# A gated linear attention layer with a convolutional FFN: the first unit ordered by need, row squares in place, and the up operands' splits later and behind loads

## The chip, the cores and the metric

The kernel runs on one core of one Trainium2 chip. The metric is the device time of one execution in microseconds; the time of a kernel is the median of its runs.

## The reference

With a depth of one, only the first mixer of the reference runs. The whole computation, in fp32, on a sequence of 2048 rows of 1024:

```
h = rmsnorm(x, mix_norm_w)
proj = h @ gla_w_in                       # 1024 -> q 512, k 512, v 1024, r 1024, gate rank 16
q, k, v, r, glr = split(proj)
log_a = log_sigmoid(glr @ w_gate2 + b_gate) / 16
g = cumsum(log_a) in chunks of 64 rows    # 4 heads, dk 128, dv 256
k_dec = k * exp(g_end - g)
for each chunk:  state = state * exp(g_end) + k_dec^T v ;  o = (q * 128**-0.5) @ state
o = rms_normalize(o) * gla_norm_w * silu(r)
x = x + o @ gla_w_out
h = rmsnorm(x, ffn_norm_w)
u = causal_dwconv(h @ w_up, conv_w, conv_b)      # 2 x 2816 columns, 3 taps
x = x + (silu(g) * val) @ w_down                 # g, val = halves of u
return rmsnorm(x, final_norm_w)
```

## The kernel before

**Arithmetic.** Every fp32 operand of a product is split into a high part (a copy to fp32r) and a low part (operand minus high part); a product is then three matmuls, high x low, low x high and high x high (`mm3p`, lines 179 to 189, matmuls at 184 to 186). `split` (191 to 194) makes the parts: the copy on ScalarE (line 193), the difference on VectorE (line 194). The large products are multiplied by blocks in seven products instead of eight, p1 to p7, which need sums and differences of blocks of both operands.

**Stages.** The rows are taken as pairs of 128-row tiles (e, d). Stage R projects r, A and B project k, q and v of two heads each and run the recurrence, Y is the output projection with the residual, U the up projection with convolution and gate, D the down projection and the last norm. One `unit(ps_, j)` is the seven products of stage `ps_` for row pair j, in the order p1, p5, p6, p2, p7, p3, p4. The host passes x a second time in transposed blocks (`xt`); each is multiplied by the norm weight on VectorE (`blocks_x`, line 461), while the factor of each row is applied after the product. That factor comes from `squares` (426): half a row tile is squared on ScalarE with its sum accumulated (line 434), and for the second half GpSimd adds the two sums (439), scales and adds epsilon (440) and takes the power -1/2 (441) into `rs`. The squares themselves go to a bf16 tile `junk` that nobody reads. Each call of `squares` issues the load of the half tile two further on (`load_rows`, 422) from ScalarE; the loads use two buffers.

**What sets the order.** The program is written down in one order; a scheduler then places each engine's instructions by that order and by when it takes operands to be ready, so an instruction written later can be issued earlier on its engine. Engines and queues run in the order placed. `tc.issue_after(ins)` places what is written in its block behind `ins` on the same engine, without waiting for it. Within the writing, a clock counts the products (`adv`, 0.227 us for a matmul of 512 columns, three to a step of `mm3p`), and `later_do(us, fn)` has `fn` written down once that clock has moved on by `us`; `need(...)` writes it down at once if it is wanted sooner.

**The first unit** (`first_pair`, 964 to 1124) does stage R for pair 0 with eight plain products, since the sums of blocks aren't there yet. SP's queue issues, in this order: the norm weight, the two transposed tiles (two halves each), the weight blocks, the 16 gate columns (`graw`, line 526, runs of 64 bytes), six copies of the second gate weight (`w2raw`, 546), its bias to all partitions (`bg`, 548), the third weight block, two further transposed tiles and two half rows. `blocks_x` for tiles 0 and 1, the masks of the recurrence (`masks`, 503) and the gate operands are written ahead of the first weight split. Then splits of weights (`weight`, 1009) and rows (`row`, 1001) alternate with products (`product`, 1060). The fourth weight block is loaded by ScalarE's queue into the buffers of the first two transposed tiles. Meanwhile `sum5`, `sum6` and `sum7` build the sums for p5, p6, p7 and p3, and `diffs` those of the rows.

**The up operands.** During the last unit of Y, after each product, `load_op(0, o)` (942) loads one operand of U for the first half of the rows, in SP's queue, in two transfers of 512 KB, and has its `halves` (950) written down `NLS` = 8.0 later by the clock: two splits of 128x1024. U itself (`phase_u`, 1254) begins when Y's last product has been written; it writes the splits of the first three up weights (`prep`, 1267; tile `uw`), then multiplies, operand by operand in the order p1, p5, p6, p7, p4, p2, p3, two column tiles each, and calls `need` for the operand before its first product.

Of the kernel before, what the change touches and what calls it, by code (L numbers as in the profile page):

```python
# [16 lines left out]
P = 128  # L17
# [8 lines left out]
def hybrid_kernel(  # L26
# [44 lines left out]
    NLY, NLE = 5.5, 9.0  # L71
    NLS = 8.0
    Y0, Y1, U0, U1 = 3.0, 2.8, 14.0, 11.0
# [117 lines left out]
    def split(hi, lo, src):  # L191

        order["act"] = nc.scalar.copy(hi, src)  # L193
        nc.vector.tensor_sub(lo, src, f32(hi))  # L194

# [228 lines left out]
    sq = {"n": 0}  # L424

    def squares():

        t, i = divmod(sq["n"], 2)
        r = xrow.pop(sq["n"])
        if i == 0:  # L430
            sq["ssq"] = small("ssq", f"ssq_a{t}", 2)
        ssq = sq["ssq"]
        junk = gp.tile([P, 1024], BF16, tag="cp", name=f"junk_{t}_{i}", bufs=4)
        nc.scalar.activation(junk[:, :512], r, AF.Square, accum_out=ssq[:, i:i + 1])
        load_rows(sq["n"] + 2, nc.scalar)
        sq["n"] += 1
        if i == 1:
            var = small("var", f"var_a{t}")
            nc.gpsimd.tensor_add(var, ssq[:, 0:1], ssq[:, 1:2])
            nc.gpsimd.tensor_scalar(var, var, 1.0 / D, EPS, op0=ALU.mult, op1=ALU.add)  # L440
            nc.gpsimd.tensor_tensor(rs[:, t:t + 1], var, neghalf, op=ALU.pow)
# [4 lines left out]
    def diff(j, o, a, c):  # L446
# [3 lines left out]
        return d  # L450

    def blocks_x(t):
        xb = xin.pop(t)
        bs = []
        for k in range(2):
            if t < 2:
                b = rp["p"].tile([P, 512], F32, tag="s2k", name=f"hb_{t}_{k}", bufs=SB)
            else:
                b = hb_tile(f"hb_{t}_{k}")
            w = nwt[:, HK * k:HK * (k + 1)].unsqueeze(2).to_broadcast([P, HK, P])  # L460
            nc.vector.tensor_tensor(b.rearrange("p (a c) -> p a c", c=P), xb[:, k, :].rearrange("p (a c) -> p a c", c=P), w, op=ALU.mult)
            bs.append(b)
        hsrc["t", t] = bs
        j = t // 2
        if t % 2 == 0:
            hsrc[j, "p1"], hsrc[j, "p2"] = bs
            return
        if j == 0:
# [32 lines left out]


    def masks():
        rp["later"] = rp["p"].tile([P, P], F32R, name="later")

        later_f = rp["p"].tile([P, 512], F32, tag="s2k", name="later_f", bufs=SB)
        nc.gpsimd.memset(later_f[:, :P], 1.0)
        nc.gpsimd.affine_select(
            out=later_f[:, :P], in_=later_f[:, :P], compare_op=ALU.is_gt, fill=0.0,
            base=0, pattern=[[-1, P]], channel_multiplier=1,  # L510
        )
        nc.gpsimd.memset(later_f[CH:P, 0:CH], 0.0)

        nc.gpsimd.memset(later_f[0:CH, CH - 1:CH], 1.0)
        nc.gpsimd.memset(later_f[CH:P, P - 1:P], 1.0)
        nc.vector.tensor_copy(rp["later"], later_f[:, :P])
        nc.vector.tensor_add(lastrow, ident[:, CH - 1:CH], ident[:, P - 1:P])

    def gate_weights():

        GR = 2 * RANK
        rp["wg"] = wg = rp["h"].tile([P, KT, GR], F32R, name="wg")
        rp["wgx"] = wgx = rp["h"].tile([P, KT, GR], F32R, name="wgx")
        graw = rp["p"].tile([P, 512], F32, tag="s2k", name="graw", bufs=SB)
        gv = graw[:, :KT * RANK].rearrange("p (a b) -> p a b", b=RANK)
        nc.sync.dma_start(gv, wv[:, :, OR + H * DV:OR + H * DV + RANK])
        nc.vector.tensor_copy(wg[:, :, :RANK], gv)
        nc.vector.tensor_sub(wg[:, :, RANK:GR], gv, f32(wg[:, :, :RANK]))

        def others():  # L530

            gx_ = graw[:, KT * RANK:2 * KT * RANK].rearrange("p (a b) -> p a b", b=RANK)
            nc.vector.tensor_add(gx_[:, :HK], gv[:, :HK], gv[:, HK:])
            nc.vector.tensor_scalar(gx_[:, HK:], gv[:, :HK], -1.0, 0.0, op0=ALU.mult, op1=ALU.add)
# [3 lines left out]
        later_do(24.0, others)  # L538

    def gate_weights2():  # L540


        rp["w2s"] = w2s = rp["p"].tile([P, 512], F32R, name="w2s")
        w2raw = rp["p"].tile([P, 512], F32, tag="s2k", name="w2raw", bufs=SB)
        for i in range(6):
            nc.sync.dma_start(w2raw[i * RANK:(i + 1) * RANK, :], w_gate2)
        rp["bg"] = rp["p"].tile([P, 512], F32, name="bg")
        nc.sync.dma_start(rp["bg"], b_gate.partition_broadcast(P))

        def parts():  # L550
            nc.vector.tensor_copy(w2s[0:96, :], w2raw[0:96, :])
# [412 lines left out]
    def first_pair():  # L964
# [17 lines left out]
        s_ = stage("p7", ((0, 0),))[:, HK:, :]  # L982
        stage("p6", ((1, 1), (1, 0)))
        fetch((0, 0))
        xin[1] = load_xt(1, 2)
        fetch((1, 0))
        gate_weights()
        gate_weights2()
        fetch((1, 1))
        xin[2], xin[3] = load_xt(2), load_xt(3)  # L990
        for m in range(2):
            load_rows(m, nc.sync)
        for t in range(2):
# [66 lines left out]
        def product(i, jj, k):  # L1060
# [38 lines left out]
        product(1, 1, 1)  # L1099
        squares()  # L1100
# [577 lines left out]
```

## Time and profile before

| what | value |
|---|---|
| median of 3 runs | 2117.09 us (2113.14 to 2125.95) |
| the profiled execution | 2119.17 us |
| its span | 2117.5 us |
| granted TensorE clock, mean | 0.994 |
| ScalarE busy, 0 to 10 us | 3.14 us |
| VectorE busy, 0 to 10 us | 1.17 us |
| transposed tiles 0 and 1, from issue to landing | 2.8 us the shortest |

A row of the timeline gives the start from the beginning of the span, the length, the engine, the line of the kernel, the operation, the tile written and the tiles read; in brackets stand the engine's idle time before it and what ended it. SPq and ACTq are transfers being issued by those two queues; PE is TensorE, PEld its weight loads, DVE VectorE, ACT ScalarE, POOL GpSimd. A row of the waits gives who waited for whom, the sum, the count and the longest. A row of a group has the count behind the x, then busy time, mean nanoseconds of one and idle time before.

### The profile page before, as it was taken

The numbers are of one execution on the slowest core, as the hardware profiler recorded it, in microseconds if no ns is written. First come the engines' busy times: TensorE is split into PE (matmuls) and PEld (weight loads), VectorE is DVE, ScalarE is ACT, GpSimd is POOL, SyncE is SP. The second block draws the span as 40 slices with busy tenths as digits, with TensorE's granted clock in tenths as the row PEclk, the third lists the DMA queues.
The fourth block names the chain that finished last, engine by engine and source line by source line (L and its number), as shares of the span: only waits on it lengthen the run. The fifth ranks groups of instructions, "written<-read, shape, count | busy, mean of one in ns | idle before, by whom it ended". The sixth has DMA issues, their size and how long they took to land.

```text
span 2117.5 us, 28200 instructions
## 1 busy us (share of the span) xinstructions
PE 2049.1 (97%) x9700; PEld 1686.1 (80%) x9700; DVE 1605.2 (76%) x2109; ACT 1109.4 (52%) x2022; POOL 672.5 (32%) x595
## 2 busy tenths in 40 slices
PE   6999999999998998999999999999999999999998
PEld 4777778878886887888888887888888788888886
DVE  7766887888878646899898867898898956566564
ACT  5656755675665666655545545445454533233342
POOL 2110000000000002555464554666766433243310
PEclk9999999999999999999999999999999999999999
DMA  8866675577858888444545376545445684454462
GB/s 293 295 219 199 223 237 178 165 247 254 292 183 267 314 271 293 155 159 136 182 139 167 132 278 204 140 110 152 122 129 148 196 322 155 144 179 164 148 218 112
DMA packets 246512, 419.32 MB, mean 198 GB/s; under 512 B 22784, under 2 KB 91520, under 8 KB 246368
## 3 DMA queue, kind: packets, MB, share of 16 engines
q1 hardware_dynamic: 203200, 335.09, 46.5%
q10 hardware_dynamic: 36832, 70.89, 9.8%
q0 software_dynamic: 6336, 11.54, 3.5%
q8 instruction: 76, 1.25, 0.2%
q14 instruction: 68, 0.56, 0.1%
HBM read 278.50 MB, written 150.47 MB: 203 GB/s over the span
## 4 chain that ended last, share of the span: by engine, by line
PE 64%; DVE 13%; POOL 7%; issue 7%; DMA 7%; ACT 2%; SPq 0%; ACTq 0%; DVEq 0%; POOLq 0%
PE pd_p L184 7%; PE pd_p L186 7%; PE pd_p L185 7%; DVE t L1315 4%; PE ua L185 4%; PE ua L184 4%; PE ua L186 3%; POOL as_p L1344 3%; DVE uw_p L194 3%; PE mp_A L184 2%; PE mp_Y L184 2%; PE mp_Y L185 2%; PE mp_Y L186 2%; PE mp_A L185 2%; PE mp_A L186 2%
## 5 line engine op out<-in xcount | busy, mean ns | idle before, releaser
L184 PE MATMUL ua<-h_p,uw_p 128*128 128x512 f32 x704 | 276.9, 393 | 10.2 <-ACT c L1297 4.5
L185 PE MATMUL ua<-h_p,uw_p 128*128 128x512 f32 x704 | 276.0, 392 | 2.8 <-DVE var_d L226 2.8
L186 PE MATMUL ua<-h_p,uw_p 128*128 128x512 f32 x704 | 275.5, 391 | 0.0
L1315 DVE SCALAR_TENSOR_TENSOR t<-u,cw,t 128x1024 f32<-128x1024 f32 x176 | 265.6, 1512 | 8.5 <-ACT t L1313 7.8
L184 PE MATMUL pd_p<-dw_p,da 128*128 128x512 f32 x616 | 239.6, 389 | 0.0
L185 PE MATMUL pd_p<-dw_p,da 128*128 128x512 f32 x616 | 239.6, 389 | 0.0
L186 PE MATMUL pd_p<-dw_p,da 128*128 128x512 f32 x616 | 239.6, 389 | 0.0
L193 ACT CAST uw_p<-us 128x512 fp32r<-128x512 f32 x132 | 82.2, 622 | 198.8 <-POOL us L1277 138.3
L194 DVE TENSOR_TENSOR da<-da_p,da 128x512 fp32r<-128x512 f32 x154 | 118.9, 826 | 87.9 <-ACT da L193 87.9
L194 DVE TENSOR_TENSOR uw_p<-us,uw_p 128x512 fp32r<-128x512 f32 x132 | 153.3, 1166 | 42.4 <-ACT uw_p L193 37.7
L194 DVE TENSOR_TENSOR uw_p<-ur,uw_p 128x512 fp32r<-128x512 f32 x176 | 146.3, 860 | 28.1 <-ACT uw_p L193 28.1
L184 PEld LDWEIGHTS ua<-h_p,uw_p 128*128 128x128 f32 x704 | 133.0, 189 | 43.2 <-ACT c L1297 8.9
L193 ACT CAST da<-da_p 128x512 fp32r<-128x512 f32 x154 | 84.7, 618 | 150.4 <-PE pd_p L186 115.3
L185 PEld LDWEIGHTS ua<-h_p,uw_p 128*128 128x128 f32 x704 | 133.0, 189 | 30.6 <-DVE uw_p L194 3.4
L186 PEld LDWEIGHTS ua<-h_p,uw_p 128*128 128x128 f32 x704 | 133.2, 189 | 27.9
L760 POOL TENSOR_TENSOR rstd<-var,pair 128x2 f32<-128x2 f32 x32 | 22.7, 709 | 410.7 <-DVE var L759 410.7
L184 PE MATMUL uc<-h_p,uw_p 128*128 128x512 f32 x352 | 137.1, 390 | 1.2 <-DMA h_p<-hd_p 1.2
L186 PE MATMUL uc<-h_p,uw_p 128*128 128x512 f32 x352 | 137.0, 389 | 0.0
L185 PE MATMUL uc<-h_p,uw_p 128*128 128x512 f32 x352 | 136.9, 389 | 0.0
L1313 ACT ACTIVATE t<-u,cw 128x1024 f32<-128x1024 f32 x88 | 109.6, 1245 | 49.9 <-DVE u L1424 49.1
L186 PEld LDWEIGHTS pd_p<-dw_p,da 128*128 128x128 f32 x616 | 115.6, 188 | 24.1
L185 PEld LDWEIGHTS pd_p<-dw_p,da 128*128 128x128 f32 x616 | 115.6, 188 | 24.1
(263 smaller groups left out, 5287.3 us busy)
## 6 DMA issues: line engine op xcount, KB each, us to landing
ur<-in_ffn_w_up_dram SPq DMA_DIRECT2D x84, 512.0 KB, 5.2
da_p<-ad_p SPq DMA_DIRECT2D x154, 256.0 KB, 4.1
ad_p<-t SPq DMA_DIRECT2D x110, 256.0 KB, 3.1
ch<-in_ffn_w_down_dram SPq DMA_DIRECT2D x61, 256.0 KB, 4.9
hr_A_p<-h1d_p SPq DMA_DIRECT2D x56, 256.0 KB, 3.3
hr_B_p<-h1d_p SPq DMA_DIRECT2D x56, 256.0 KB, 3.2
hr_Y_p<-yd_p SPq DMA_DIRECT2D x56, 256.0 KB, 3.9
hd_p<-h2p_p ACTq DMA_DIRECT2D x56, 256.0 KB, 2.1
```

Of the source, the lines that this page charges most:

```text
L184: nc.tensor.matmul(ps_ap, ah, bl, start=(first and i == 0), stop=False, **kw)
L185: nc.tensor.matmul(ps_ap, al, bh, start=False, stop=False, **kw)
L186: nc.tensor.matmul(ps_ap, ah, bh, start=False, stop=(last and i == len(pairs) - 1), **kw)
L193: order["act"] = nc.scalar.copy(hi, src)
L194: nc.vector.tensor_sub(lo, src, f32(hi))
L760: nc.gpsimd.tensor_tensor(rstd, var, neghalf.to_broadcast([P, 2]), op=ALU.pow)
L1313: nc.scalar.activation(t, u[:, 2:2 + TS], AF.Identity, scale=cw[:, 2, c:c + 1], bias=cw[:, 3, c:c + 1])
L1315: nc.vector.scalar_tensor_tensor(t, u[:, k:k + TS], cw[:, k, c:c + 1], t, op0=ALU.mult, op1=ALU.add)
L1344: upool["ins"] = nc.gpsimd.tensor_add(av, last if x is None else x, y)
```

## The change

In the first unit, every transposed half tile is loaded, normed and split one at a time, as its product needs it; the loads on SP alternate with the weight blocks; the gate columns, the second gate weight and its bias are issued by ScalarE's queue instead of SP's; VectorE's and ScalarE's instructions are chained to one order with `issue_after`; masks and gate operands are written after the first weight blocks. `squares` writes over the row tile it reads, with the scale 1/sqrt(1024) inside, and VectorE adds the two sums and epsilon in one instruction; GpSimd keeps the power. Half rows 2 to 5 get buffers of their own (the `cp` tiles, where `junk` was) and are loaded by SP in front. For U, `NLS` becomes 11.0, and each split of `halves` is placed behind the ScalarE copy of the split last written.

```diff
-    NLS = 8.0
+    NLS = 11.0
...
         order["act"] = nc.scalar.copy(hi, src)
-        nc.vector.tensor_sub(lo, src, f32(hi))
+        order["dve"] = nc.vector.tensor_sub(lo, src, f32(hi))
...
     def load_rows(m, q):
         t, i = divmod(m, 2)
+        sq["ahead"] = m + 1
         if t < NTT:
-            xrow[m] = rp["h"].tile([P, 512], F32, tag="xr", name=f"xr_{t}_{i}", bufs=2)
+            if 2 <= m < 6:
+                xrow[m] = cp_tile(f"xr_{t}_{i}")
+            else:
+                xrow[m] = rp["h"].tile([P, 512], F32, tag="xr", name=f"xr_{t}_{i}", bufs=2)
...
-        junk = gp.tile([P, 1024], BF16, tag="cp", name=f"junk_{t}_{i}", bufs=4)
-        nc.scalar.activation(junk[:, :512], r, AF.Square, accum_out=ssq[:, i:i + 1])
-        load_rows(sq["n"] + 2, nc.scalar)
+        nc.scalar.activation(r, r, AF.Square, scale=float(D) ** -0.5, accum_out=ssq[:, i:i + 1])
+        if sq["n"] not in (2, 3, 4, 5):
+            load_rows(sq["ahead"], nc.scalar)
         sq["n"] += 1
         if i == 1:
             var = small("var", f"var_a{t}")
-            nc.gpsimd.tensor_add(var, ssq[:, 0:1], ssq[:, 1:2])
-            nc.gpsimd.tensor_scalar(var, var, 1.0 / D, EPS, op0=ALU.mult, op1=ALU.add)
+            nc.vector.scalar_tensor_tensor(var, ssq[:, 0:1], EPS, ssq[:, 1:2], op0=ALU.add, op1=ALU.add)
             nc.gpsimd.tensor_tensor(rs[:, t:t + 1], var, neghalf, op=ALU.pow)
...
+    last = {}
+
+    def behind(e):
+        return tc.issue_after(last[e].ins) if e in last else ExitStack()
...
-        nc.sync.dma_start(gv, wv[:, :, OR + H * DV:OR + H * DV + RANK])
-        nc.vector.tensor_copy(wg[:, :, :RANK], gv)
-        nc.vector.tensor_sub(wg[:, :, RANK:GR], gv, f32(wg[:, :, :RANK]))
+        nc.scalar.dma_start(gv, wv[:, :, OR + H * DV:OR + H * DV + RANK])
+
+        def plain():
+            with behind("dve"):
+                nc.vector.tensor_copy(wg[:, :, :RANK], gv)
+                last["dve"] = nc.vector.tensor_sub(wg[:, :, RANK:GR], gv, f32(wg[:, :, :RANK]))
...
         for i in range(6):
-            nc.sync.dma_start(w2raw[i * RANK:(i + 1) * RANK, :], w_gate2)
+            nc.scalar.dma_start(w2raw[i * RANK:(i + 1) * RANK, :], w_gate2)
...
-        nc.sync.dma_start(rp["bg"], b_gate.partition_broadcast(P))
+        nc.scalar.dma_start(rp["bg"], b_gate.partition_broadcast(P))
...
             def halves():
                 for v in vs:
-                    split(t[:, 0, v, :], t[:, 1, v, :], f32(t[:, 1, v, :]))
+                    with tc.issue_after(order["act"].ins):
+                        split(t[:, 0, v, :], t[:, 1, v, :], f32(t[:, 1, v, :]))
...
+        xb = [raw_tile([P, 2, 512], f"xt_{t}") for t in range(2)]
+
+        def fetch_x(t, k):
+            nc.sync.dma_start(xb[t][:, k:k + 1, :], xt[t][:, k:k + 1, :])
+
+        fetch_x(0, 0)
         fetch((0, 0))
-        xin[1] = load_xt(1, 2)
+        fetch_x(1, 0)
         fetch((1, 0))
-        gate_weights()
+        fetch_x(0, 1)
+        fetch_x(1, 1)
+        fetch((1, 1))
+        gate_plain_w = gate_weights()
         gate_weights2()
-        fetch((1, 1))
         xin[2], xin[3] = load_xt(2), load_xt(3)
-        for m in range(2):
+        for m in range(6):
             load_rows(m, nc.sync)
-        for t in range(2):
-            blocks_x(t)
-        masks()
-        nc.gpsimd.memset(halo, 0.0)
...
+        def norm(t, k):
+            b[k, t] = d = rp["p"].tile([P, 512], F32, tag="s2k", name=f"hb_{t}_{k}", bufs=SB)
+            with behind("dve"):
+                last["dve"] = scaled(d, xb[t][:, k, :], k)
+
+        def first_split(hi, lo, src):
+            with behind("act"):
+                last["act"] = nc.scalar.copy(hi, src)
+            with behind("dve"):
+                last["dve"] = nc.vector.tensor_sub(lo, src, f32(hi))
...
+        norm(0, 0)
+        row(0, 0)
         weight("p1", (0, 0), "p1")
-        row(0, 0)
+        norm(1, 0)
         row(0, 1)
+        gate_plain_w()
         weight("p3", (1, 0))
+        masks()
+        nc.gpsimd.memset(halo, 0.0)
         product(0, 0, 0)
         gate_plain(j, 0, 0, *h[0, 0])
+        norm(0, 1)
         row(1, 0)
         product(0, 0, 1)
         gate_plain(j, 0, 1, *h[0, 1])
         weight("p4", (1, 1), "p4")
+        norm(1, 1)
         row(1, 1)
...
-        squares()
         product(1, 0, 0)
         squares()
+        squares()
         product(1, 0, 1)
+        weight("p2", (0, 1), "p2")
         squares()
-        weight("p2", (0, 1), "p2")
         squares()
         product(1, 1, 0)
         gate_plain(j, 1, 0, *h[1, 0])
         blocks_x(2)
         blocks_x(3)
+        squares()
         product(1, 1, 1)
         squares()
```

Sums, differences and the remaining gate and mask instructions of the first unit are put `behind("dve")` or behind the last split in the same way; the last two `squares` of the unit move one place.

More of the change, by code (lines that the diff above doesn't have):

```diff
@@ L450, in diff, with scaled @@
         return d
+    def scaled(dst, src, k):
+        w = nwt[:, HK * k:HK * (k + 1)].unsqueeze(2).to_broadcast([P, HK, P])
+        return nc.vector.tensor_tensor(dst.rearrange("p (a c) -> p a c", c=P), src.rearrange("p (a c) -> p a c", c=P), w, op=ALU.mult)
     def blocks_x(t):
@@ L455, in blocks_x @@
         for k in range(2):
[L456 to L461, printed above, removed]
+            b = hb_tile(f"hb_{t}_{k}")
+            with behind("dve"):
+                scaled(b, xb[:, k, :], k)
             bs.append(b)
@@ L466, in blocks_x @@
             hsrc[j, "p1"], hsrc[j, "p2"] = bs
-            return
-        if j == 0:
             return
@@ L515, in masks @@
         nc.gpsimd.memset(later_f[CH:P, P - 1:P], 1.0)
-        nc.vector.tensor_copy(rp["later"], later_f[:, :P])
-        nc.vector.tensor_add(lastrow, ident[:, CH - 1:CH], ident[:, P - 1:P])
+        with behind("dve"):
+            nc.vector.tensor_copy(rp["later"], later_f[:, :P])
+            nc.vector.tensor_add(lastrow, ident[:, CH - 1:CH], ident[:, P - 1:P])
     def gate_weights():
@@ L525, in gate_weights @@
         gv = graw[:, :KT * RANK].rearrange("p (a b) -> p a b", b=RANK)
-        nc.sync.dma_start(gv, wv[:, :, OR + H * DV:OR + H * DV + RANK])
-        nc.vector.tensor_copy(wg[:, :, :RANK], gv)
-        nc.vector.tensor_sub(wg[:, :, RANK:GR], gv, f32(wg[:, :, :RANK]))
+        nc.scalar.dma_start(gv, wv[:, :, OR + H * DV:OR + H * DV + RANK])
[3 more added lines that the diff above has]
+                last["dve"] = nc.vector.tensor_sub(wg[:, :, RANK:GR], gv, f32(wg[:, :, :RANK]))
         def others():
             gx_ = graw[:, KT * RANK:2 * KT * RANK].rearrange("p (a b) -> p a b", b=RANK)
-            nc.vector.tensor_add(gx_[:, :HK], gv[:, :HK], gv[:, HK:])
-            nc.vector.tensor_scalar(gx_[:, HK:], gv[:, :HK], -1.0, 0.0, op0=ALU.mult, op1=ALU.add)
+            with behind("dve"):
+                nc.vector.tensor_add(gx_[:, :HK], gv[:, :HK], gv[:, HK:])
+            with behind("dve"):
+                nc.vector.tensor_scalar(gx_[:, HK:], gv[:, :HK], -1.0, 0.0, op0=ALU.mult, op1=ALU.add)
             nc.vector.tensor_copy(wgx[:, :, :RANK], gx_)
@@ L538, in gate_weights @@
         later_do(24.0, others)
+        return plain
     def gate_weights2():
@@ L545, in gate_weights2 @@
         for i in range(6):
-            nc.sync.dma_start(w2raw[i * RANK:(i + 1) * RANK, :], w_gate2)
+            nc.scalar.dma_start(w2raw[i * RANK:(i + 1) * RANK, :], w_gate2)
         rp["bg"] = rp["p"].tile([P, 512], F32, name="bg")
-        nc.sync.dma_start(rp["bg"], b_gate.partition_broadcast(P))
+        nc.scalar.dma_start(rp["bg"], b_gate.partition_broadcast(P))
         def parts():
-            nc.vector.tensor_copy(w2s[0:96, :], w2raw[0:96, :])
+            with behind("dve"):
+                nc.vector.tensor_copy(w2s[0:96, :], w2raw[0:96, :])
             nc.vector.tensor_sub(w2s[64:96, :], w2raw[64:96, :], f32(w2s[64:96, :]))
@@ L1003, in row @@
             t = w_pair(f"h_{ps_}{j}_{i}{k}")
-            split(t[:, 0, :], t[:, 1, :], b[i, k])
+            first_split(t[:, 0, :], t[:, 1, :], b[i, k])
             if o:
@@ L1013, in weight @@
                 v = (slice(None), slice(2 * k, 2 * k + 2))
-                split(hi[v], lo[v], need_raw[ij][k] if isinstance(need_raw[ij], list) else need_raw[ij][v])
+                first_split(hi[v], lo[v], need_raw[ij][k] if isinstance(need_raw[ij], list) else need_raw[ij][v])
             if key:
@@ L1031, in sum5 @@
             for k in range(2):
-                nc.vector.tensor_add(s_[V[k]], a21[V[k]], a22[V[k]])
+                with behind("dve"):
+                    nc.vector.tensor_add(s_[V[k]], a21[V[k]], a22[V[k]])
             split_sum("p5", [s_[V[k]] for k in range(2)])
@@ L1038, in sum6 @@
             for k in range(2):
-                nc.vector.tensor_sub(xsum[V[k]], a11[V[k]], a21[V[k]])
+                with behind("dve"):
+                    nc.vector.tensor_sub(xsum[V[k]], a11[V[k]], a21[V[k]])
             split_sum("p6", [s_[V[k]] for k in range(2)])
@@ L1048, in diffs @@
             sub, put = nc.vector.tensor_sub, nc.sync.dma_start
-            sub(b[0, 0], b[0, 1], b[0, 0])
+            with tc.issue_after(order["dve"].ins):
+                sub(b[0, 0], b[0, 1], b[0, 0])
             put(h1d[j, "p5"], b[0, 0])
-            sub(b[0, 1], b[1, 1], b[0, 1])
+            with tc.issue_after(order["dve"].ins):
+                sub(b[0, 1], b[1, 1], b[0, 1])
             put(h1d[j, "p7"], b[0, 1])
@@ L1106, in first_pair @@
         product(0, 1, 0)
+        squares()
         prep_rows(len(PORD) + 2)
         sum6()
-        squares()
         product(0, 1, 1)
-        squares()
         later_do(22.0, diffs)
@@ L1537, in hybrid_kernel @@
     nc.sync.dma_start(nwt, mix_norm_w)
-    xin[0] = load_xt(0, 2)
     first_pair()
```

8 lines of the change are left out of this document (4 added, 4 removed).

## Prediction

> **What bounds the kernel now.** I read the page's busy shares first, then TensorE's waits over the whole span, then windows, and last the timeline, engine by engine, where TensorE stands still.
>
> ```profile
> span 2117.5 us, 28200 instructions
> PE 2049.1 (97%) x9700; PEld 1686.1 (80%) x9700; DVE 1605.2 (76%) x2109; ACT 1109.4 (52%) x2022; POOL 672.5 (32%) x595
> ...
> PE m_R L184 <- ACT h_R L193: 14.7, 1, 14.7
> ...
> PE ua L184 <- ACT uw_p L193: 3.1, 1, 3.1
> ...
> PE ua L185 <- DVE var_d L226: 2.8, 1, 2.8
> ```
>
> TensorE is the bound: 2117.5 - 2049.1 = 68.4 us idle is all that a change of order can win. The change touches two places: the start (14.7 us before the first product) and the passage from the output projection to the up projection (3.1 + 2.8). Windows (columns: length, PE, PEld, DVE, ACT, POOL, granted clock, DMA share, GB/s):
>
> ```profile
> 10.00:20.00 10.00, 4.24 (x9) 3.06 (x10) 9.66 (x16) 5.16 (x8) 0.00 (x0) 1.00 0.84 247
> 20.00:30.00 10.00, 10.00 (x56) 8.15 (x56) 10.00 (x12) 4.69 (x8) 1.67 (x1) 1.00 1.04 400
> 30.00:40.00 10.00, 10.00 (x57) 8.23 (x56) 7.38 (x15) 5.36 (x11) 4.23 (x6) 1.00 0.93 305
> 40.00:50.00 10.00, 8.73 (x43) 6.54 (x41) 9.91 (x11) 7.48 (x16) 5.96 (x6) 1.00 0.75 278
> 50.00:60.00 10.00, 6.83 (x34) 5.10 (x34) 9.95 (x14) 8.90 (x15) 1.82 (x2) 1.00 0.83 265
> ...
> 820.00:840.00 20.00, 14.12 (x51) 10.75 (x50) 16.43 (x19) 12.45 (x16) 6.98 (x5) 0.83 1.02 413
> 840.00:860.00 20.00, 20.00 (x97) 16.39 (x96) 15.23 (x18) 18.66 (x39) 8.54 (x7) 1.00 0.36 121
> 860.00:880.00 20.00, 20.00 (x90) 16.54 (x90) 19.14 (x18) 8.89 (x14) 13.21 (x11) 1.00 0.23 85
> ```
>
> From 10 to 60 us VectorE is busy 46.9 us of 50: that stretch has two bounds close together. An earlier TensorE start is worth only as much as VectorE can follow.
>
> **The start.** Timeline rows (start, length, engine, line):
>
> ```profile
> 1.74 0.45 ACTq L1542 DMA_DIRECT2D cw<-in_ffn_conv_w_dram  x1
> ...
> 2.23 1.28 ACT L193 ACT_TABLE_LOAD   x1 [2.23 <-issue]
> ...
> 6.21 0.52 SPq L526 DMA_DIRECT2D graw<-in_gla_w_in_dram  x1
> 6.77 3.19 SPq L546 DMA_DIRECT2D w2raw<-in_gla_w_gate_dram  x1
> ...
> 7.92 1.04 ACT L193 CAST w_R_p<-ws_p 128x1024 fp32r<-128x1024 f32 x1 [4.41 <-DMA ws_p<-in_gla_w_in_dram]
> 8.99 2.50 DVE L194 TENSOR_TENSOR w_R_p<-ws_p,w_R_p 128x1024 fp32r<-128x1024 f32 x2 [7.31 <-ACT w_R_p L193]
> ...
> 12.93 1.29 DVE L461 TENSOR_TENSOR hb<-xt,nwt 128x512 f32<-128x512 f32 x2
> 13.11 0.36 SPq L548 DMA_DIRECT2D bg<-in_gla_b_gate_dram  x1
> ...
> 13.63 0.90 SPq L980 DMA_DIRECT2D ws_p<-in_gla_w_in_dram  x2
> ...
> 14.07 0.61 ACT L193 CAST h_R<-hb 128x512 fp32r<-128x512 f32 x1
> ...
> 15.81 1.29 DVE L194 TENSOR_TENSOR h_R<-hb,h_R 128x512 fp32r<-128x512 f32 x2
> ...
> 16.55 0.79 PE L185 MATMUL m_R<-w_R_p,h_R 128*128 128x512 f32 x1 [1.03 <-DVE h_R L194]
> ```
>
> The first weight half has its low part at 8.99 + 2.50/2 = 10.24, but the row operand is normed only at 12.93, cast at 14.07, and regular products run from 16.55; less one step (0.45 at half pace, twice the 0.227 of the program's own clock), that is a start at 16.1. In the new order norm, cast and low part of the first row (1.29/2, 0.61, 1.29/2) come before the weights, while they load. If the weights' cast starts no later than 7.92, products start at 10.24: a TensorE gain of 16.1 - 10.24 = 5.9 us.
>
> What may make it later is ScalarE's queue. Three transfers are issued there now (0.4 us each), and the table load follows at 2.23. Eight more go in front: graw, six w2raw, bg. At 0.45 us each that puts the table load at 2.23 + 8 x 0.45 = 5.8 and its end at 7.1, just in time. But transfers wait for one another: bg goes out at 13.11, when the eighth transfer before it (the second half of the second weight block) has landed, and the next weights at 13.63, where graw lands (its last figure is the time from issue to landing; the second row is w2raw's):
>
> ```profile
> graw<-in_gla_w_in_dram SPq DMA_DIRECT2D x1, 64.0 KB, 7.4
> ...
> DMA to landing us min/median/max: 2.7/3.5/7.0
> ```
>
> 6.21 + 7.4 = 13.61. If that holds over both queues, the fourth w2raw waits on ScalarE for graw, and what is behind it, the old three transfers, the table load and all casts, waits as well. With graw issued near 0.8 (two issues of 0.45 before 1.74) and landing 4 us later (an estimate between w2raw's median and graw's 7.4, the queue being empty), that is 4.8; the first of the old three waits for that w2raw, 2.7 at the shortest, so 7.5; two more issues 0.9, table load 1.28, row cast 0.61: the weights' cast begins at 10.3, 2.4 us late, and the gain is 3.5. The same move frees SP: the last weight block, two transfers of 512 KB, can go out before 13.63.
>
> The Trainium skill, "DMA: Bandwidth & Descriptors", section "Issuing engines are not separate DMA queues", says that transfers issued on different engines share the same 16 engines and only the issuing time is saved. By it the 64 + 192 + 256 KB moved to ScalarE's queue would take turns with the first weights; at the 247 GB/s of 10 to 20 us that is 2.1 us, an estimate, and the gain would be 3.8 instead of 5.9.
>
> VectorE's side: it starts its dense stretch at 8.99 now. The change takes the first row's norm and low part (1.3 us) ahead of it, could fill the 3.1 us idle between 10 and 60, and adds one small instruction per norm factor:
>
> ```profile
> L226 DVE TENSOR_SCALAR var_d<-ssq_d x16: 142/154/155, 694.3 to 838.3; 128x1 f32<-128x1 f32 x16
> ...
> 47.79 1.22 DVE L194 TENSOR_TENSOR w_R_p<-ws_p,w_R_p 128x1024 fp32r<-128x1024 f32 x1
> ...
> 52.48 0.50 PE L184 MATMUL mp_R<-w_R_p,h_R_p 128*128 128x512 f32 x1 [2.51 <-ACT cp_R L1211]
> ```
>
> The nearest row for that instruction is 0.154 us; six fall before 60 us: 0.9 us. VectorE thus leads by 1.3 - 0.9 = 0.4 us (idle stays) to 3.5 (idle gone), or, with casts 2.4 us late, by -2.0 to 1.1. The last low part of p6's weights ends at 47.79 + 1.22 = 49.0 while TensorE starts p6 at 52.48 because ScalarE is late with a copy; that is 3.5 us of slack, so VectorE permits 1.5 to 7.0. The smaller of the two sides: 1.5 to 5.9. I take **4.0**, since ScalarE's copies, queued before 52.48, need not move all the way up.
>
> **Squares and norm factor.** ScalarE now waits for rows and GpSimd does three steps:
>
> ```profile
> ACT junk L434 <- DMA xr<-in_x_dram: 8.2, 6, 2.8
> ...
> L439 POOL TENSOR_TENSOR var_a<-ssq_a 128x1 f32<-128x1 f32 x10 | 10.4, 1044 | 84.6 <-ACT junk L434 81.3 <-ACT dec L633 3.3
> ```
>
> Six rows loaded ahead remove most of those 8.2 us from ScalarE, four of them in SP's queue, past which the rows' stores move by 4 x 256 KB = 2.6 us at the 400 GB/s of 20 to 30; those stores are read back only for stage A. Two GpSimd steps (the first 1.04 us in the mean) vanish from the way to rs; the power stays. All of it is hidden behind products, and counts nothing beyond the start's 4.0: it is part of why ScalarE can follow. If that cover went, it would be the 0.15 us per factor, 16 x 0.15 = 2.4. Squares in place write fp32 where they wrote bf16; the nearest row, the cast of 14.07, writes as many four-byte numbers in 0.61 us, so I take zero. The masks move from GpSimd's first 3 us into its idle 10 to 30, and with the gate operands and diffs they only change places on VectorE.
>
> **The passage to the up projection.**
>
> ```profile
> 827.71 0.39 PE L186 MATMUL mp_Y<-w_Y_p,h_Y_p 128*128 128x512 f32 x1
> 831.18 1.02 PE L184 MATMUL ua<-h_p,uw_p 128*128 128x512 f32 x2 [3.09 <-ACT uw_p L193]
> 834.97 0.79 PE L185 MATMUL ua<-h_p,uw_p 128*128 128x512 f32 x1 [2.77 <-DVE var_d L226]
> ...
> 828.38 2.23 ACT L193 CAST h_p<-h_p 128x1024 fp32r<-128x1024 f32 x2 [0.56 <-DMA h_p<-hz_p]
> ...
> 830.52 1.13 ACT L193 CAST uw_p<-ur 128x512 fp32r<-128x512 f32 x2
> ...
> 829.19 0.69 DVE L1199 TENSOR_TENSOR x<-x,mp_Y 128x512 f32<-128x512 f32 x1
> 829.79 3.93 DVE L194 TENSOR_TENSOR h_p<-h_p 128x1024 fp32r<-128x1024 f32 x2
> ...
> 834.24 0.68 DVE L194 TENSOR_TENSOR uw_p<-ur,uw_p 128x512 fp32r<-128x512 f32 x1
> ```
>
> The first up weights are cast at 830.52, behind four operands' splits; their low part follows the 3.93 us of such splits. In the program's clock a product is 12 x 0.227 = 2.72 and the last unit 19.07. With 8.0 the splits fall due at 10.7, 13.4, 16.2, 18.9: four before the unit ends and the first up weights are written down. With 11.0 they fall due at 13.7, 16.4, 19.2, 21.9: two before. Queueing each behind the split last written keeps the others behind those weights also where a load seems ready. So the cast of 830.52 can be done before 828, the idle 3.09 + 2.77 = 5.86 goes, and with it the slowed clock: 0.83 granted over 20 us is 3.4 us at half pace, 1.7 lost. In full: 7.6 us. At least one thing stays possible: the low part behind the add of 829.19, ending near 830.5, with 2.4 us idle left: 5.2 us. Two operands' splits (p6, p2; four of 1.2 to 2.0 us on VectorE, 4.8 to 7.9) move into the up projection, where VectorE is busy 15.2, then 19.1 of 20 us; 4.8 us of the first window and 0.9 of the second are free for them. Between 0 and 7.9 - 5.6 = 2.3 is given back. Between 5.2 and 7.6, less 1.0: **5.4**, bounds 2.9 to 7.6; the p6 product, 4 x 2.72 = 10.9 us on, is when the moved work is first missed.
>
> **Sum:** 4.0 + 5.4 = 9.4 us, bounds 4.4 to 13.5. The profiled execution took 2119.2 (span 2117.5 and 1.7 around it), so 2109.8 for such a one; the median of the runs, 2117.1, is 2.1 below it: **2107.7**.
>
> **Rivals.**
> - Both places give all they have: 5.9 + 7.6 = 13.5, time 2103.6. For it: ScalarE has idle time in both. Against: two queues must fall out ideally.
> - VectorE holds the start: the first units end when they end now. For it: 9.91 and 9.95 of 10 busy at 40 to 60. Against: the 3.5 us of slack at 52.48. Only 5.4 is left: 2111.7.
> - The passage gives back what it wins, because the moved splits meet a full VectorE; then only 4.0: 2113.1. For it: 19.14 of 20. Against: 4.8 us free just before. The Trainium skill, "SBUF — State Buffer", "Only the shared port pair causes contention", has a VectorE instruction with two SBUF inputs and a reading GpSimd one block each other. The pair of 3.93 us against 2.36 elsewhere agrees with it.
> - Slower: ScalarE stuck issuing. If graw, issued near 0.8, lands 7.4 us later (8.2), the fourth w2raw's issue takes 3.2 us more, as the first's does at 6.77, and lands 7.0 later (18.4), and the three old transfers wait for it (19.8), then table load and first row's cast end at 21.7; weights are cast 13.8 us late, products start at 10.24 + 13.8 = 24.0, 7.9 later than 16.1. With 5.4 won at the passage, 2.5 us slower: 2119.6. It decides from a weight cast at 7.92 + 5.9 + 5.4 = 19.2. Against: the three old ones may well be put behind the casts, and graw meets little traffic at 0.8.
>
> **Chances and range.** Forecast 0.45; both in full 0.17; VectorE holds the start 0.15; given back 0.13; ScalarE stuck 0.10. The range runs from 3 us below the full case to just short of the stuck one, since the new order also shifts instructions elsewhere and the three runs spread over 12.8 us: 2100 to 2118. A measurement of this kernel tells about 1%, 21 us, from no change. No case wins 21 us and none loses them; I leave 0.05 for faster, as 20.2 us are idle before 60 (10 + 5.76 + 1.27 + 3.17 by the windows) and much of them could go, and 0.03 for slower.
>
> **What would show it.** Right: first product between 10 and 13 us, no idle over 1 us before the fourth; the second unit's p6 near 48; the first up product within 2.5 us of the last output product and a granted clock above 0.9 from 820 to 840 (shifted by the start's gain). Wrong: casts on ScalarE beginning after 13 us, waits of several us between 35 and 55 on VectorE's low parts, or new TensorE waits from 830 to 900. It is wrong altogether if the gain at those two places is there and the end is not 5 to 13 us earlier.

## The result and the profile after

The changed kernel takes **2129.8 us** in the median (2124.1 to 2139.9), the kernel before 2117.7 beside it (14 runs each): a ratio of **1.0056, 95% interval 1.0044 to 1.0069**. It is slower by about 12 us, outside the predicted range, though within the 1% that the prediction named as its bound for no change. Its profiled execution took 2129.7 (span 2128.0).

The page and TensorE's waits after (who waited for whom: total us, times, longest):

```profile
span 2128.0 us, 28195 instructions
PE 2055.6 (97%) x9700; PEld 1691.2 (79%) x9700; DVE 1604.9 (75%) x2125; ACT 1109.3 (52%) x2022; POOL 653.1 (31%) x563
```

```profile
PE m_R L184 <- DVE w_R_p L1028: 11.3, 1, 11.3
PE ua L184 <- ACT c L1337: 8.2, 8, 2.9
PE pe L646 <- ACT e L655: 7.1, 4, 4.2
...
PE pz L631 <- DVE w2s L567: 5.9, 1, 5.9
PE mp_R L184 <- ACT cp_R L1251: 4.4, 2, 3.6
PE ua L185 <- DVE var_d L226: 2.8, 1, 2.8
```

The first wait fell from 14.7 to 11.3, and the 3.1 on `uw_p` is gone. New ones stand in the first units: on the gate's second weight (`pz`, 5.9), its decay (`pe`, 7.1) and a copy (`cp_R`, 3.6). The windows of after, then those of before from 60 us on (columns as in the prediction):

```profile
20.00:40.00 20.00, 19.83 (x99) 16.01 (x97) 14.52 (x23) 13.12 (x28) 6.58 (x4) 1.00 0.87 309
40.00:60.00 20.00, 13.64 (x58) 10.69 (x59) 20.00 (x26) 14.87 (x28) 1.20 (x1) 0.83 0.59 210
60.00:80.00 20.00, 14.12 (x71) 11.14 (x70) 13.61 (x25) 8.32 (x20) 1.51 (x3) 0.83 0.91 311
80.00:100.00 20.00, 17.91 (x97) 14.16 (x96) 15.19 (x29) 15.88 (x31) 3.19 (x5) 1.00 1.00 346
100.00:120.00 20.00, 15.79 (x77) 12.66 (x75) 9.17 (x17) 11.43 (x31) 2.62 (x4) 0.91 0.70 247
```

```profile
60.00:80.00 20.00, 18.19 (x96) 14.88 (x97) 16.41 (x26) 11.24 (x22) 4.25 (x6) 1.00 1.01 352
80.00:100.00 20.00, 20.00 (x115) 16.28 (x114) 13.00 (x21) 12.95 (x29) 2.96 (x6) 1.00 0.78 274
100.00:120.00 20.00, 20.00 (x112) 16.55 (x111) 11.03 (x18) 9.88 (x22) 2.79 (x6) 1.00 0.71 235
```

From 40 to 120 us TensorE is idle 6.4 + 5.9 + 2.1 + 4.2 = 18.5 us after, against 4.4 + 1.8 = 6.3 before: 12.3 us more. The granted clock is at 0.83, 0.83 and 0.91 where it was 1.00; that is (0.17 + 0.17 + 0.09) x 20 = 8.6 us of full clock lost, part of it while TensorE is idle anyway. Between 60 and 80 us neither VectorE (13.6 of 20) nor ScalarE (8.3) is full: something waits. These rows group ScalarE's instructions from 0 to 120 us (count | busy, mean ns | idle time just before them and its cause), after first, then before:

```profile
L437 ACT ACTIVATE xr<-xr 128x512 f32<-128x512 f32 x32 | 20.1, 629 | 26.7 <-DMA xr<-in_x_dram 24.6 <-DVE hb L457 1.4 <-DVE var_a L443 0.5
```

```profile
L434 ACT ACTIVATE junk<-xr 128x512 bf16<-128x512 f32 x20 | 12.5, 627 | 12.9 <-DMA xr<-in_x_dram 12.9
```

All 32 squares now run in the first 120 us instead of 20, and ScalarE stands still 24.6 us for their rows instead of 12.9. One square costs the same (629 against 627 ns). In the timeline of after the chain reads so (start, length):

```profile
73.20 0.63 ACT L437 ACTIVATE xr<-xr 128x512 f32<-128x512 f32 x1 [4.33 <-DMA xr<-in_x_dram]
73.83 0.34 ACT L614 CAST gstk<-pg 32x256 fp32r<-32x256 f32 x1
...
74.21 0.41 DVE L615 TENSOR_TENSOR gstk<-pg,gstk 32x256 fp32r<-32x256 f32 x1 [4.14 <-ACT gstk L614]
74.65 0.68 DVE L567 TENSOR_TENSOR w2s<-w2raw,w2s 32x512 fp32r<-32x512 f32 x1
75.39 1.22 PE L631 MATMUL pz<-w2s,gstk 96*128 96x512 f32 x2 [5.88 <-DVE w2s L567]
```

A square waits 4.33 us for its row; the gate's copy stands behind it on ScalarE; VectorE waits 4.14 us for that copy and has its low part of `w2s` next; TensorE waits 5.88 us for this. TensorE's row names VectorE, but the delay comes from a row load, two engines back. In the same way a square that waited for its row stands in front of a copy at 42.7 us (TensorE waits 2.72) and of an Exp at 106.1 (4.21).

How far the products are ahead or behind is read from the starts of TensorE's matmuls: that of the nth, minus the nth's of before, in us. The second column is the time in before; the others are after and six kernels of the next section.

| n | before | after | squares held | in place alone | in place held | first unit alone | no up part | up part alone |
|---|---|---|---|---|---|---|---|---|
| 0 | 14.7 | -3.4 | -3.2 | 0.0 | -0.2 | -3.8 | -3.4 | 0.0 |
| 125 | 41.5 | -5.2 | -4.4 | 0.3 | -0.3 | -5.3 | -3.9 | 0.7 |
| 175 | 56.5 | -0.4 | 0.9 | 0.7 | 1.2 | -1.5 | 0.1 | 1.1 |
| 275 | 77.0 | 4.8 | -1.6 | 11.4 | 0.2 | -1.2 | 7.0 | -0.1 |
| 325 | 86.9 | 7.3 | 0.0 | 12.4 | 0.5 | 0.5 | 10.3 | 0.4 |
| 400 | 99.9 | 13.3 | 0.0 | 18.2 | 5.7 | 1.9 | 15.3 | 0.4 |
| 2350 | 476.1 | 8.8 | -7.4 | 14.6 | -1.0 | 0.9 | 7.5 | -5.1 |
| 4100 | 818.9 | 8.4 | -8.3 | 14.6 | -2.5 | 0.9 | 8.1 | -5.4 |
| 4150 | 838.5 | 4.3 | -13.6 | 14.5 | -2.8 | 0.9 | 8.1 | -11.8 |
| 4250 | 860.0 | 9.5 | -7.6 | 14.6 | -2.5 | 0.9 | 8.1 | -3.3 |
| 9699 | 2108.7 | 10.2 | -11.9 | 10.9 | -2.5 | -0.4 | 8.2 | -7.9 |

After leads by 5.2 us until 42 us, loses 18.5 by 100 us, wins 4.1 at the passage and loses 5.2 behind it. The last column is a measure of how finely this can be read: up to the last output unit that kernel has the order of before on every engine, and its profiled execution still drifts to 5.4 us ahead by n = 4100. So steps of several us within one stretch count here, slow drifts of five do not. Where the text names other numbers of n, or other kernels, they are read in the same way.

### The profile page after: what moved, and what is told of

Read it like the earlier page. It is cut to its first block, busy times and chain, and to the rows that moved or that the text cites. A ratio compares the mean times of both kernels' runs of the same rounds, so it can differ in the third digit from the quotient of the medians.

```text
span 2128.0 us, 28195 instructions
## 1 busy us (share of the span) xinstructions
PE 2055.6 (97%) x9700; PEld 1691.2 (79%) x9700; DVE 1604.9 (75%) x2125; ACT 1109.3 (52%) x2022; POOL 653.1 (31%) x563
## 4 chain that ended last, share of the span: by engine, by line
PE 61%; DVE 13%; issue 7%; POOL 7%; DMA 7%; ACT 4%; SPq 0%; ACTq 0%; DVEq 0%; POOLq 0%
PE pd_p L186 7%; PE pd_p L185 7%; PE pd_p L184 7%; DVE t L1355 4%; PE ua L184 3%; PE ua L185 3%; PE ua L186 3%; DVE uw_p L194 3%; POOL as_p L1384 3%; PE mp_B L184 2%; PE mp_A L184 2%; PE mp_Y L184 2%; PE mp_Y L185 2%; PE mp_Y L186 2%; PE mp_B L185 2%
## 5 line engine op out<-in xcount | busy, mean ns | idle before, releaser
L184 PE MATMUL ua<-h_p,uw_p 128*128 128x512 f32 x704 | 277.4, 394 | 10.3 <-ACT c L1337 8.2
L1355 DVE SCALAR_TENSOR_TENSOR t<-u,cw,t 128x1024 f32<-128x1024 f32 x176 | 260.3, 1481 | 7.6 <-ACT t L1353 6.9
L184 PEld LDWEIGHTS ua<-h_p,uw_p 128*128 128x128 f32 x704 | 133.0, 189 | 43.1 <-ACT c L1337 13.3
```

The source lines that it names most:

```text
L184: nc.tensor.matmul(ps_ap, ah, bl, start=(first and i == 0), stop=False, **kw)
L1355: nc.vector.scalar_tensor_tensor(t, u[:, k:k + TS], cw[:, k, c:c + 1], t, op0=ALU.mult, op1=ALU.add)
```

## The experiments

**The theory after the result:** `junk` was one of four `cp` tiles, shared with the units' copies. So a square could not run before an earlier copy had given up its tile; that would have kept squares near their unit. In place, nothing holds them, and ScalarE's order has them far in front, two at a time behind row loads. **The rivals:** the write in place is itself dear; the new order of the first unit makes the loss; the up part does.

**1. In place alone**: the kernel before with one line changed.

```
-        junk = gp.tile([P, 1024], BF16, tag="cp", ...)
-        nc.scalar.activation(junk[:, :512], r, AF.Square, accum_out=ssq[:, i:i + 1])
+        nc.scalar.activation(r, r, AF.Square, accum_out=ssq[:, i:i + 1])
```

> The kernel before, with the squares written over their row tile and nothing else (two row buffers, the old loads, three GpSimd steps). Squares run ahead: slower, as 20 squares instead of 12 stand before the first table load on ScalarE; 3 to 10 us, ratio 1.0015 to 1.005, with TensorE waits between 60 and 115 us. Late gate weights: no pins here, so no difference, ratio 1.000 within 0.001.

Measured: 2130.0 us, ratio 1.0064 (1.0046 to 1.0082) to the 2117.8 of the kernel before beside it; 12 us, more than the 3 to 10 expected. One line makes the whole loss: 18 us behind by the 400th product. Its ScalarE from 0 to 120 us:

```profile
L433 ACT ACTIVATE xr<-xr 128x512 f32<-128x512 f32 x31 | 19.5, 630 | 30.6 <-DMA xr<-in_x_dram 30.5
```

**2. Squares held**: the changed kernel, and from the ninth square on each is placed behind the ScalarE copy of the split written last.

```
+        with tc.issue_after(order["act"].ins) if sq["n"] >= 8 else ExitStack():
             nc.scalar.activation(r, r, AF.Square, ...)
```

> The changed kernel, with each square from the ninth on placed behind the ScalarE copy of the split last written. Theory (squares run ahead): nothing but their bf16 tile held the squares near their unit; without it they are issued up to 74 us early and ScalarE, in order, waits for their rows (24.6 us instead of 12.9). Held, the waits go, the 18.5 us lost between 36 and 113 us go for the most part, and the kernel takes 2110 to 2117, ratio to the kernel before 0.997 to 1.000. Rival (late gate weights): TensorE's 5.9 us wait for the second gate weight comes from the pins on VectorE; it stays, and the ratio stays at 1.004 or above.

Measured: **2111.1 us, ratio 0.9976 (0.9959 to 0.9993)**. ScalarE's 24.6 us of waits for rows fell to 2.5, with the same squares in place:

```profile
L438 ACT ACTIVATE xr<-xr 128x512 f32<-128x512 f32 x21 | 13.2, 627 | 2.5 <-DMA xr<-in_x_dram 2.5
```

It beats both kernels. It was run a second time.

> The same kernel as the run with held squares, beside the one with the later difference: ratio to before 0.996 to 0.999, TensorE's wait at p6 of the first two units near 5.7 us, and no lead at the 325th matmul.

Measured: 2113.0, ratio 0.9986 (0.9975 to 0.9997); TensorE's wait at p6 was 5.7 us, and products led by 0.2 us at the 325th. From 1.0056 to 0.9976 and 0.9986 holding is worth 0.0080 and 0.0070 of 2117 us: 17 and 15 us.

**3. In place, held**: the kernel before with both edits, of 1 and of 2.

> The kernel before with squares in place, and from the ninth square on each placed behind the split written last. Theory (the loss comes from the order that ScalarE gets, not from writing fp32 in place): no lag over 2 us at the 400th matmul, time 2114 to 2120 instead of the 2130.0 of squares in place alone. Rival (the write in place itself, or the row buffer that it keeps, costs): 2126 or more.

Measured: 2117.2, ratio 0.9997 (0.9980 to 1.0015). Writing in place costs nothing; the order does. From 0 to 120 us ScalarE has as many squares as before, at the same cost, and waits less for their rows (8.2 us against 12.9):

```profile
L434 ACT ACTIVATE xr<-xr 128x512 f32<-128x512 f32 x20 | 12.6, 629 | 8.2 <-DMA xr<-in_x_dram 8.2
```

At the 400th product it lagged by 5.7 us where the theory allowed 2: an Exp of the gate came 3.6 us late, behind another gate operand's cast that waited 5.9 us for a transfer.

**4. First unit alone**: the change without the squares' edits (bf16 tile, three GpSimd steps, two row buffers) and without its up part.

> The changed kernel with only its new order of the first unit: squares write the bf16 tile as before, GpSimd keeps three steps, two row buffers, up splits due at 8.0 and not placed behind one another. Theory (in-place squares make the whole loss, the order of the first unit gains at the start): products lead by 4 to 5 us at the 125th matmul, no lag of 18 us at the 400th, time 2110 to 2116. If VectorE takes the gain back, as in the run with held squares, the lead is below 1 us at the 325th matmul and the time is 2115 to 2119. Rival (the first unit's order itself makes the loss): a lag over 8 us at the 400th matmul and 2125 or more.

Measured: 2116.6, ratio 0.9994 (0.9983 to 1.0006). The start gains 5.3 us until the 125th product and has none of it at the 325th. That is the size that the expectation named, but VectorE is not what takes most of it here. By the 155th product, ahead of p6, 5.1 us are gone (timeline):

```profile
38.13 0.63 ACT L435 ACTIVATE junk<-xr 128x512 bf16<-128x512 f32 x1 [4.41 <-DMA xr<-in_x_dram]
...
42.63 0.31 PE L601 MATMUL pg<-h_R_p,wg 128*32 128x128 f32 x1 [2.88 <-ACT gstk L614]
```

The sixth square, with its bf16 tile, waits 4.41 us for its row; a weight's cast and the gate's `gstk` stand behind it, TensorE waits 2.88 us, and the granted clock is 0.50 from 42.0 to 48.8. So a square in front of needed work costs time here too, although `junk` is there. In the run with squares held, where half rows 2 to 5 have buffers of their own, products still lead by 4.7 us at the 155th; there the lead goes at p6 (timeline):

```profile
45.49 2.35 DVE L1071 TENSOR_TENSOR xsum<-ws_p,ws_p 128x1024 f32<-128x1024 f32 x2
...
49.74 2.35 DVE L194 TENSOR_TENSOR w_R_p<-ws_p,w_R_p 128x1024 fp32r<-128x1024 f32 x2
...
47.88 1.99 ACT L193 CAST w_R_p<-ws_p 128x1024 fp32r<-128x1024 f32 x2 [3.63 <-DVE xsum L1071]
...
51.01 0.80 PE L184 MATMUL mp_R<-w_R_p,h_R_p 128*128 128x512 f32 x1 [5.73 <-DVE w_R_p L194]
```

p6's low part ends at 52.1. In the kernel before it ended at 49.0, and the difference for p7 (`xsum`) had been taken long before (timeline):

```profile
11.79 1.23 DVE L1039 TENSOR_TENSOR xsum<-ws_p,ws_p 128x1024 f32<-128x1024 f32 x1 [0.29 <-DMA ws_p<-in_gla_w_in_dram]
...
20.49 1.22 DVE L1039 TENSOR_TENSOR xsum<-ws_p,ws_p 128x1024 f32<-128x1024 f32 x1
```

The change moved these two instructions to 45.49, ahead of p6, while VectorE now idles 5.5 us between 20 and 40 in the changed kernel (2.6 before), 4.1 of them for ScalarE's casts and 1.6 for a square.

**5. The difference later**: squares held, and `xsum` written behind p6's split, without a chain.

```
+            split_sum("p6", [s_[V[k]] for k in range(2)])
             for k in range(2):
-                with behind("dve"):
-                    nc.vector.tensor_sub(xsum[V[k]], a11[V[k]], a21[V[k]])
-            split_sum("p6", [s_[V[k]] for k in range(2)])
+                nc.vector.tensor_sub(xsum[V[k]], a11[V[k]], a21[V[k]])
```

> The changed kernel with held squares, and in the first unit the difference for p7's weights (two subtractions of 1.2 us on VectorE) written behind p6's split instead of ahead of it. In the run with held squares VectorE did it at 45.5, ScalarE waited 3.6 us for it with p6's casts, and TensorE then waited 5.7 us for p6's low part at 51.0. Theory (VectorE's order of the first unit takes back the start's gain): p6 starts 2.3 to 3.6 us earlier, products lead the kernel before by 1.5 to 3 us at the 325th matmul (0.0 in the run with held squares), time 2 to 3 us below that run's in the same job. Rival (VectorE is full until 60 us whatever the order): the wait moves to p7's low parts, no lead at the 325th matmul, the same time.

Measured: 2119.3, ratio 1.0018 (1.0008 to 1.0027): slower. The wait at p6 went from 5.73 to 0.72 us, as the theory had it, but the unchained difference came out far ahead instead of behind, at the head of VectorE's queue (timeline):

```profile
12.95 1.23 DVE L1072 TENSOR_TENSOR xsum<-ws_p,ws_p 128x1024 f32<-128x1024 f32 x1 [3.10 <-DMA ws_p<-in_gla_w_in_dram]
...
49.05 0.50 PE L184 MATMUL mp_R<-w_R_p,h_R_p 128*128 128x512 f32 x1 [0.72 <-ACT cp_R L1252]
```

There it waits 3.10 us for its block, the first low part behind it waits too, and the first product starts at 15.4: the whole start is lost. It is the squares' mistake once more, on VectorE. That alone doesn't make the run slower: with the wait at p6 gone, products lead the kernel before by 3.1 us at the 175th and 3.4 at the 275th, where squares held lags by 0.9 and leads by 1.6. Then they fall behind, by 0.6 at the 325th (1.5 to 3 ahead was expected) and 5.6 at the 400th (timeline):

```profile
93.80 0.62 ACT L193 CAST lh<-e 128x512 fp32r<-128x512 f32 x1 [5.54 <-DMA ed<-e]
...
94.96 0.66 PE L647 MATMUL pe<-ident,e 128*128 128x128 f32 x4 [3.25 <-ACT e L656]
```

A gate operand's cast waits 5.54 us for a transfer, an Exp stands behind it, and TensorE waits 3.25 us for that; run 3 has the same cast with a wait of 5.93. So VectorE's order decides p6; that the start's gain can be kept in the end isn't shown. The difference chained behind p6's low part wasn't tried.

**6. The up part.** The change without it (splits due at 8.0, no chain), and the kernel before with nothing else:

> The changed kernel with the up operands' splits as before (8.0, not queued behind the last split). If the up part gives back what it wins (4.1 won at the passage, 5.2 lost within 40 us after it), the time stays within 2 us of the changed kernel, ratio 1.005 to 1.006. If the up part wins the 5.4 of the forecast and the loss after the passage has another cause, this is 4 to 6 us slower still, ratio 1.008.

Measured: 2127.9, ratio 1.0052 (1.0037 to 1.0067).

> The kernel before with the up part alone (11.0, each split behind the ScalarE copy of the split last written). Given back: within 2 us of the kernel before, ratio 0.999 to 1.001, first up product without ScalarE's wait, and a new wait for the copy of the first up product some 30 us later. Forecast: 5.4 us faster, ratio 0.9975.

Measured: 2115.4, ratio 0.9991 (0.9977 to 1.0005). By the table the up part wins 6.4 us between the 4100th and 4150th product and gives 8.5 back by the 4250th; without it both stretches are level. And the change with held squares, without it:

> The changed kernel with held squares and without its up part (splits due at 8.0, not placed behind one another). By matmul numbers the up part won 5.2 us and gave 6.0 back in the run with held squares. Theory (give-back on ScalarE's copy cancels it): the same time within 2 us, 2109 to 2113. Rival (my prediction's 5.4 us are kept in net): 2115 to 2118.

Measured: 2114.2, ratio 0.9987 (0.9974 to 1.0000) against 0.9976 and 0.9986 with it; it lies between the two ranges expected. In net the up part lies between 2 us lost (2127.9 without it, 2129.8 with it) and 3 won (2114.2 and 2111.1), not told apart from nothing.

**7. Splits later still**: squares held, `NLS` 14.0.

> The changed kernel with each square held behind the last split written (as in the run with held squares) and the splits of the up projection due at 14.0 instead of 11.0. In the run with held squares the matmul numbers 4100 to 4150 gained 5.2 us and numbers 4150 to 4250 lost 6.0 again, where TensorE waited 2.9 us for the ScalarE copy of p6 behind a 2.00 us split. Theory (the give-back is the copy behind the moved splits): another 2.7 us later takes this split past the copy, the idle of 2.9 us and most of the loss of 6.0 go, time 2106 to 2109 against 2111.1. Rival (whatever is moved later meets the next copy or VectorE, which is full there): the wait only changes its place, time 2110 to 2113. Rival 2 (the splits come too late for their own products): waits on h_p, slower than 2113.

Measured: 2113.7, ratio 0.9980 (0.9967 to 0.9993). The wait of 2.9 us on the copy at p7's first product is gone, as the theory had it (the 2.1 below stands later, at 886.6). But p5's first product now waits 4.1 us for the low part of its own `h_p`, a moved split:

```profile
PE uc L184 <- DVE h_p L194: 4.1, 1, 4.1
PE ua L184 <- ACT c L1338: 2.5, 2, 2.1
```

Between the 4100th and the 4150th product it won 8.4 and by the 4250th gave 7.4 back. The pause at p5, with the granted clock at 0.50 from 828.4 to 835.2 behind it, is all of what was given back. That is the second rival's mechanism: moved this far, a split comes too late for its own product. The ratio does not differ from that of squares held (0.9976 and 0.9986), so it costs about what the first one did.

## Why the prediction was wrong, point by point

**Squares and norm factor: this step failed.** The prediction said that "All of it is hidden behind products, and counts nothing beyond the start's 4.0". It priced the instruction (0.61 us, and 629 against 627 ns is right) and its loads, and even had the ScalarE waits for rows shrink from 8.2 us. It did not ask what else the removed tile did. `junk` shared four buffers with the units' copies, and once it is gone the squares run ahead of their units, in front of work that TensorE needs. By runs 1 to 3 this costs 12 to 17 us (12 by run 1 alone, 14 by run 1 against run 3, 15 and 17 by run 2), more than the 9.4 us that were to be won. None of the rivals had it: the slower one put ScalarE's trouble at 0 to 20 us, in issuing. The list of what would show the prediction wrong looked for waits between 35 and 55 us on VectorE's low parts; they came between 43 and 107, mostly on what stood behind squares.

**The start: right in itself, and then the third case.** Rows of after:

```profile
8.98 1.04 ACT L1026 CAST w_R_p<-ws_p 128x1024 fp32r<-128x1024 f32 x1
...
11.33 0.80 PE L184 MATMUL m_R<-w_R_p,h_R 128*128 128x512 f32 x1 [11.33 <-DVE w_R_p L1028]
```

The weights' cast begins at 8.98, not at 10.3 or 19.2: the three old transfers went behind the casts, so ScalarE did not get stuck. Products lead by 5.2 us, between the 4.0 taken and the bound of 5.9, with no idle before the fourth. But the p6 bound was read wrongly: "3.5 us of slack, so VectorE permits 1.5 to 7.0" took p6's low part to move forward with the rest, and the instructions that the new order moves to "only change places on VectorE". Two of them, 2.35 us, were moved from its early stretch to just ahead of that low part, which ends at 50.8 in the changed kernel and at 52.1 with squares held, against 49.0 before. The rival "VectorE holds the start" is right in its sum (run 4: 5.3 us ahead, then level) and wrong in its reason: VectorE was not full, it idles 5.5 us between 20 and 40. What took the lead was order, of a square on ScalarE in run 4 and of the difference on VectorE with squares held; run 5, with the difference out of the way, leads at p6.

**The passage: won, and given back elsewhere than named.** Rows of after:

```profile
836.16 0.39 PE L186 MATMUL mp_Y<-w_Y_p,h_Y_p 128*128 128x512 f32 x1
836.38 0.61 PE L184 MATMUL ua<-h_p,uw_p 128*128 128x512 f32 x2
837.99 0.67 DVE L1239 TENSOR_TENSOR x<-x,mp_Y 128x512 f32<-128x512 f32 x1
838.59 1.16 DVE L194 TENSOR_TENSOR uw_p<-ur,uw_p 128x512 fp32r<-128x512 f32 x1
839.80 0.50 PE L185 MATMUL ua<-h_p,uw_p 128*128 128x512 f32 x1 [2.80 <-DVE var_d L226]
...
860.26 2.00 ACT L193 CAST h_p<-h_p 128x1024 fp32r<-128x1024 f32 x2
862.16 0.59 ACT L1337 COPY c<-ua 128x512 f32<-128x512 f32 x1
862.80 0.50 PE L184 MATMUL ua<-h_p,uw_p 128*128 128x512 f32 x1 [2.92 <-ACT c L1337]
```

The first up product follows at once; the wait on `uw_p`'s cast is gone. The "one thing" that "stays possible" came as described: the low part behind the last add, 2.80 us idle. So 4.1 to 6.4 us are won by the 4150th product, near the 5.4. Then a moved split of 2.00 us stands on ScalarE in front of p6's copy, and p7's first product waits 2.92 us: 5.2 to 8.5 us given back. The prediction had seen that the moved splits must run somewhere, but counted room on VectorE alone; the copy on ScalarE, busy 18.66 of 20 us there before, was the nearer bound. The rival "gives back what it wins" is right in its sum and wrong in its place.

The slowed clock (1.7 us in the sum) was counted as won with the idle time; it was not. It was also misread: 0.83 granted over 20 us is 6.8 us at half pace, not 3.4, and lies from 832.5 to 839.3, partly in the pauses. Short stretches of before, then of after, the last row with squares held:

```profile
834.00:836.00 2.00, 1.03 (x3) 0.84 (x4) 1.58 (x4) 0.00 (x0) 0.93 (x1) 0.50 1.01 414
836.00:838.00 2.00, 2.00 (x6) 1.61 (x5) 0.00 (x0) 1.98 (x2) 0.00 (x0) 0.50 1.04 413
838.00:840.00 2.00, 2.00 (x7) 1.54 (x7) 0.85 (x2) 1.58 (x4) 0.98 (x2) 0.66 0.93 365
```

```profile
836.00:840.00 4.00, 1.20 (x6) 0.70 (x5) 4.00 (x5) 0.26 (x2) 3.23 (x3) 1.00 1.03 422
840.00:841.00 1.00, 1.00 (x4) 0.81 (x4) 0.41 (x1) 0.15 (x1) 0.82 (x1) 0.73 1.02 410
841.00:842.00 1.00, 1.00 (x3) 0.72 (x3) 0.00 (x0) 1.00 (x2) 0.00 (x0) 0.50 1.01 406
842.00:844.00 2.00, 2.00 (x6) 1.58 (x5) 0.52 (x2) 1.58 (x5) 0.55 (x1) 0.53 1.04 422
864.40:867.70 3.30, 3.30 (x10) 2.54 (x9) 3.02 (x6) 2.61 (x6) 0.00 (x0) 0.50 0.55 168
```

```profile
823.10:830.00 6.90, 6.90 (x33) 5.73 (x34) 2.06 (x4) 5.48 (x7) 2.79 (x3) 1.00 1.02 415
```

The sign asked for, a clock above 0.9 from 820 to 840, is met at 1.00 and says nothing: half pace begins after 840, behind the pause. Before, products ran at about half the clock from 835.0 to 839.3; after, from 840.5 to 843.9. The one pause of 2.80 us draws 3.4 us of slow running, the two of before 4.3; the pause of 2.92 at p7 draws another 3.4, from 864.4. So the slow running grew, from 4.3 to 6.8 us, and at half pace it costs half of that. The Trainium skill, "TensorE: Matmul & The Clock Gate", section "What's actually happening", has an activity window of about 3.4 us that runs on its own and halves the clock after an idle one. The slow stretches of after agree in length; the pauses of 2.80 and 2.92 us are shorter than such a window, and there the measurement decides. Nor does the length of a pause settle it: with squares held the same pause of 2.80 us ends at 823.05, and the clock behind it is granted at 1.00. What decides it isn't shown.

**The shared port.** The low part at 838.59 took 1.16 us where it takes 0.68 elsewhere, and GpSimd was busy 3.23 of those 4 us; GpSimd's `ur<-ur` ran beside it until 839.20. That agrees with the contention that the prediction cited beside the pair of 3.93 us; it is one row, and no run separates it.

**What stays open.** Why ScalarE's order in runs 3 and 5 puts a cast that waits for a transfer in front of an Exp of the gate; and whether the part of the loss that after regains between the 400th and the 2350th product (13.3 to 8.8) is more than the drift that two executions of one order show.

## What to carry to other kernels

Before a scratch tile is removed, ask what its ring made wait: a buffer that looks like waste may be what keeps an instruction near its place, and an instruction fed by a load, set free on an in-order engine, blocks all that stands behind it until its data lands. Give such work an explicit place (here one line, 14 to 17 us), and count its cost on the queue it stands in, not by its own length. When work is moved out of a gap, follow it to the place where it now stands, on each engine it uses.

## What the runs showed of the hardware that was not expected

- After a pause of 2.80 us TensorE ran at full pace for 0.7 us, then at half (0.50 and 0.53 granted) until 843.9; the window that holds the pause shows 1.00. With squares held and in run 5, pauses of 2.80 and 2.81 us at the same place drew no slow stretch, while in the kernel before pauses of 1.95 and 1.80 us were followed by 3.4 us at 0.50, from 313.7 and from 436.6.
- Two executions whose engines have the same order until then can stand 5.4 us apart after 819 us (the last column of the table). The two slow stretches from 313.7 and 436.6 stand in one and not in the other; an estimate of their cost is half of 3.4 us, 1.7 each. So two single profiles of this kernel do not tell 0.2% apart; medians of 9 to 14 runs come with intervals of 0.1 to 0.2% to each side.
